# Down projection as seven block products in a hybrid-mixer layer on one core

## The chip, the core and the metric

The kernel runs on one core of a Trainium2 chip, as one program. Its engines are TensorE (PE, with PEld for its weight loads), VectorE (DVE), ScalarE (ACT), GpSimd (POOL) and the queue of SyncE (SP), which issues the DMAs of the kernel. The metric is the device time of one execution in microseconds, the median of several runs; lower is better.

## The reference

One layer of a diffusion backbone with 1024 tokens and 1024 channels: modulated norm, three token mixers (window attention, global attention, a two-way recurrence), a gated merge, an output projection, and then a gated feed-forward part with a depthwise convolution. What the change touches is the last product:

```python
def conv_ffn(h, w_up, w_dw, b_dw, w_down):
    a, g = jnp.split(dwconv(h @ w_up, w_dw, b_dw), 2, axis=-1)
    return (a * jax.nn.silu(g)) @ w_down          # (1024, 2816) @ (2816, 1024)
...
x = x_mix + m_lat[:, :, 5] * conv_ffn(h, ...)
return rms_norm(x, norm_final)
```

Everything is in float32.

## The kernel before

**Number format.** A float32 operand of a product is split into a high part, rounded to the fp32r format of TensorE, and a low part, the rest. A product is then three matmuls: high by high, high by low, low by high (`dn`, lines 982 to 985). The high part is a cast on ACT, the low part a subtraction on DVE (`split`, lines 735 to 737, for activations; `w_unit`, lines 155 to 168, for weights).

**Who sets the order.** The program is written as straight code; a planner then orders the instructions of each engine by a priority, which is the place in the code, lowered by an offset where `tc.high_priority(offset)` stands. It takes whatever is ready with the lowest number and puts in the semaphores. Tiles of one tag share a few buffers, and an instruction that needs a buffer waits until its last reader is done. Each engine then runs its own list in order. Weights go through three tags with three buffers each (`WR`, `WH`, `WL`): `wr` the raw float32 tile, `wh` and `wl` its two parts. Loads and stores are issued on SP.

**Global attention** (`attention` with `br` = 1, lines 1287 to 1427, in stage lines 683 to 691). Sixteen iterations `it`, one for 128 tokens and four heads. In iteration `it` three pieces of work are interleaved on PE: the scores of iteration `it + 1` (`softmax_global`, line 1469), the values of iteration `it` (`values`, line 1355: transposes `pp` of the probabilities, their split `ph` and `pl`, products `po`), and a filler, the gate projections (`gz`), whose weights come through `w_unit`. POOL has one instruction in an iteration: it copies the reciprocals of the softmax sums, widened, into a tile `rb` (line 1504, kept in `rs`). Two matmuls of `values` read that tile (`pr`, line 1372).

**Up projection** (lines 824 to 953). It is already done as seven block products for each pair of column tiles (Strassen's scheme in Winograd's form), with sums of weights made on POOL (lines 889 to 896). The activations that come out, 22 tiles of 128 by 1024, are stored to DRAM (`act_d`).

**Down projection** (lines 959 to 1077). The 2816 rows of the weights are 22 row tiles f, the 1024 output channels are 8 column tiles, the 1024 tokens two halves `tb`. The first half is done in two passes over all f (four column tiles in each, in four PSUM banks), the second half in one such pass and then column tile by column tile, with the last column tile cut into 384 and 128 tokens (`LAST`), so that the final norm of the first piece runs beside the matmuls of the second. In a pass a weight unit holds two row tiles by 512 columns, so that PE does 24 matmuls for one unit. Activations are loaded as half tiles `st` (four buffers), split, and the parts kept in a ring of 25 places (`ac`), from which both passes of the first half read. When a pass is done, DVE adds the PSUM banks, scaled, to the residual tile `xt` (`out_tile`), ACT squares the result, and POOL or DVE adds the squares for the final norm (`sumsq`).

## Time and profile before

| | |
|---|---|
| median of 3 runs | 2111.61 us (2109.61 to 2113.57) |
| the profiled execution, its own time | 2108.34 us |
| its span, first to last instruction | 2106.5 us |
| PE, PEld busy | 2068.0 us (98%), 1730.7 us (82%) |
| DVE, ACT, POOL busy | 1375.5, 1000.8, 287.1 us |
| granted TensorE clock | 0.998 of full speed |
| global attention | about 890 to 1190 us from the start of the span |
| up projection | 1415 to 1844 us |
| down projection | 1844 us to the end |

The profile is one execution, with all times counted from the first instruction. A row of the timeline has the start, the duration, the engine, the line of the code, the operation, the tile written and the tiles read, the shape, and in brackets how long the engine stood idle before it and what ended that. Durations of matmuls overlap, since they are pipelined: the distance of their starts is the pace. A row of a tile has the shortest, median and longest duration in nanoseconds, and the first and the last start. In a row of stretches stand the length, the busy time of each engine with its number of instructions, the granted clock, the share of the DMA engines' time and GB/s.

### The profile page before, as it was taken

Reading aid. Unit: us, or ns where it says so; the run is one execution under the profiler, and the core shown is the slowest. Engines: PE = TensorE matmul, PEld = TensorE weight load, DVE = VectorE, ACT = ScalarE, POOL = GpSimd, SP = SyncE. Lnnn points to the kernel's source line nnn. Section 1 sums busy time; section 2 is a strip of 40 time slices with the busy share of each in tenths; the row PEclk is TensorE's granted clock in tenths of the full one; section 3 lists DMA queues with packets and bytes.
Section 4 is the critical chain, followed back from the end, with each engine's and each line's share of the span. In section 5 each row is a group of like instructions: output and inputs, shape, how many; then the busy total and the mean of one; then the engine's idle time right before and its main releaser. Section 6 shows DMA issues by size and latency. Waiting matters only on the chain.

```text
span 2106.5 us, 30452 instructions
## 1 busy us (share of the span) xinstructions
PE 2068.0 (98%) x11666; PEld 1730.7 (82%) x11666; DVE 1375.5 (65%) x2280; ACT 1000.8 (48%) x1749; POOL 287.1 (14%) x257
## 2 busy tenths in 40 slices
PE   8999999999999999999999999999999999999997
PEld 5888888888988888778888788878888888888887
DVE  4846656636675788588888747569777777664423
ACT  4333333311123877688888634346544454453322
POOL 0000000010021222100000000011333334100111
PEclk9999999999999999999999999999999999999999
DMA  9311111136544211311010454641222222295342
GB/s 370 133 45 37 35 51 41 46 126 210 185 143 139 78 51 48 96 33 36 32 32 28 153 179 141 201 150 59 92 80 80 90 80 81 83 310 191 106 122 85
DMA packets 94338, 225.48 MB, mean 107 GB/s; under 512 B 10608, under 2 KB 35568, under 8 KB 93168
## 3 DMA queue, kind: packets, MB, share of 16 engines
q1 hardware_dynamic: 94192, 223.53, 32.0%
q8 instruction: 92, 1.51, 0.3%
q14 instruction: 54, 0.44, 0.1%
HBM read 177.88 MB, written 45.61 MB: 106 GB/s over the span
## 4 chain that ended last, share of the span: by engine, by line
PE 70%; DVE 2%; ACT 2%; issue 1%; POOL 1%; DMA 1%; SPq 0%; DVEq 0%; ACTq 0%; POOLq 0%
PE pp L1377 4%; PE gz L188 3%; PE gz L189 3%; PE dn L984 3%; PE dn L985 3%; PE dn L983 3%; PE gz L190 3%; PE up L907 2%; PE up L909 2%; PE up L908 2%; PE po L1363 2%; PE po L1364 2%; PE br L189 2%; PE br L190 2%; PE br L188 2%; PE upc L909 2%
## 5 line engine op out<-in xcount | busy, mean ns | idle before, releaser
L164 ACT CAST wh<-wr 128x1024 fp32r<-128x1024 f32 (+1 forms) x139 | 145.1, 1045 | 394.8 <-PE dn L984 72.6
L165 DVE TENSOR_TENSOR wl<-wr,wh 128x1024 fp32r<-128x1024 f32 (+1 forms) x139 | 171.2, 1232 | 217.6 <-ACT wh L164 214.4
L1382 DVE TENSOR_TENSOR pl<-pp,ph 128x512 fp32r<-128x512 f32 x236 | 159.7, 688 | 29.4 <-ACT ph L1381 23.7
L188 PE MATMUL gz<-hh,wh 128*128 128x512 f32 x384 | 155.4, 405 | 2.9 <-ACT gs L578 2.9
L189 PE MATMUL gz<-hl,wh 128*128 128x512 f32 x384 | 151.7, 395 | 0.0
L190 PE MATMUL gz<-hh,wl 128*128 128x512 f32 x384 | 151.6, 395 | 0.0
L1381 ACT CAST ph<-pp 128x512 fp32r<-128x512 f32 x236 | 135.5, 585 | 32.0 <-PE pp L1377 29.2
L199 PE MATMUL tm<-wl,hh 128*128 128x256 f32 x384 | 108.9, 283 | 2.4 <-DVE wl L165 2.4
L198 PE MATMUL tm<-wh,hh 128*128 128x256 f32 x384 | 108.7, 283 | 0.0
L200 PE MATMUL tm<-wh,hl 128*128 128x256 f32 x384 | 108.6, 283 | 0.0
L1363 PE MATMUL po<-ph,VHL 128*128 128x512 f32 x236 | 106.2, 450 | 1.5 <-ACT ph L1381 1.1
L984 PE MATMUL dn<-ac,wh 128*128 128x512 f32 x256 | 99.7, 390 | 0.0
L985 PE MATMUL dn<-ac,wl 128*128 128x512 f32 x256 | 99.6, 389 | 0.0
L983 PE MATMUL dn<-ac,wh 128*128 128x512 f32 x256 | 99.6, 390 | 0.0
L1364 PE MATMUL po<-pl,VHL 128*128 128x512 f32 x236 | 97.6, 413 | 0.1
L188 PEld LDWEIGHTS gz<-hh,wh 128*128 128x128 f32 x384 | 72.3, 188 | 16.3 <-ACT gs L578 5.0
L190 PEld LDWEIGHTS gz<-hh,wl 128*128 128x128 f32 x384 | 72.2, 188 | 15.0
L189 PEld LDWEIGHTS gz<-hl,wh 128*128 128x128 f32 x384 | 72.5, 189 | 11.2
L1377 PE MATMUL pp<-ident,plat 128*128 128x128 f32 x512 | 76.6, 273 | 0.0
L1377 PEld LDWEIGHTS pp<-ident,plat 128*128 128x128 f32 x512 | 62.8, 140 | 16.9 <-DVE pl L1382 1.2
L199 PEld LDWEIGHTS tm<-wl,hh 128*128 128x128 f32 x384 | 73.7, 192 | 3.3 <-DVE wl L165 3.0
L188 PE MATMUL br<-yh,wh 128*128 128x512 f32 x192 | 74.3, 390 | 1.2 <-ACT yh L1522 1.2
(1419 smaller groups left out, 5862.8 us busy)
## 6 DMA issues: line engine op xcount, KB each, us to landing
wr<-in_w_cm SPq DMA_DIRECT2D x48, 512.0 KB, 3.8
wr<-in_w_up SPq DMA_DIRECT2D x44, 512.0 KB, 3.5
wr<-in_w_down SPq DMA_DIRECT2D x33, 512.0 KB, 3.6
wmr<-in_w_mod SPq DMA_DIRECT2D x32, 512.0 KB, 4.6
gate_d<-gs SPq DMA_DIRECT2D x48, 256.0 KB, 2.1
sgt<-gate_d SPq DMA_DIRECT2D x24, 512.0 KB, 3.5
act_d<-u SPq DMA_DIRECT2D x22, 512.0 KB, 2.6
st<-act_d SPq DMA_DIRECT2D x44, 256.0 KB, 4.2
```

Source lines behind the costliest of these rows:

```text
L164: A.copy(hi[:, :n], raw[:, :n])
L165: (lo_eng or V).tensor_tensor(out=lo[:, :n], in0=raw[:, :n], in1=hi[:, :n].bitcast(F32), op=ALU.subtract)
L188: T.matmul(psl, wh[:, k, c], hh[:, k0 + k, cols], start=s, stop=False)
L189: T.matmul(psl, wh[:, k, c], hl[:, k0 + k, cols], start=False, stop=False)
L190: T.matmul(psl, wl[:, k, c], hh[:, k0 + k, cols], start=False, stop=e)
L199: T.matmul(psl, hh[:, k, toks], wl[:, k % 4, :], start=False, stop=False)
L983: T.matmul(z, w[0][:, c], h[0], start=s, stop=False)
L984: T.matmul(z, w[0][:, c], h[1], start=False, stop=False)
L985: T.matmul(z, w[1][:, c], h[0], start=False, stop=e)
L1363: T.matmul(po, vv, ph, start=n == 0, stop=False)
L1377: T.transpose(pp[:, h], PT(h, n), ident)
L1382: V.tensor_tensor(out=pl, in0=pp, in1=ph.bitcast(F32), op=ALU.subtract)
```

## The change

The down projection becomes seven products of blocks of half the size in each dimension: 11 row tiles, four column tiles, 512 tokens. With activations A and weights W in four blocks each, the products are, in this order, A11 with W11 (into PSUM set 0), a sum of activations with a sum of weights `T1` (into set 1), A12 with W21 (on top of set 0), another with the sum `22` (on top of set 1), one with `T2` (set 0 anew), one with `T3` (set 1 anew), and one with the plain block `T4`, which goes column tile by column tile as the second half did before. After each of the first six, DVE adds the set, scaled, to one, two or three groups of four residual tiles (`after`), so that both residual halves are in use from the first product on.

The sums of weights don't depend on the data. They are made in the global attention: after each iteration a step of the generator `down_sums` adds up on POOL what the last step loaded, stores the four results to DRAM (`s_d`) from POOL's queue, takes one `wr` and one `wl` buffer, writes one column of each from the tile `rb` of the next iteration, and loads the four blocks of the next row tile into them, on POOL's queue too.

The sums of activations are made on POOL in the down projection, in place, in raw tiles that stay in SBUF: 33 raw half tiles (15 in `p2`, 8 in `pa`, 10 in the five buffers of the tag `c`), and 11 more (`r`) that go through two buffers of the tag `st`. The split parts go through a ring of 12 places. The two weight arrays of the down projection become one, `w_dn`, cut into blocks with rows of 512 columns; an input that was not read, and a debugging output, are gone.

```diff
+        s_d = dt_([4, KD, P, 512], "s_d")
+        def down_sums():
+            last = None
+            turn = yield
+            for k in range(KD + 1):
+                if last is not None:
+                    (a11, a12), (a21, a22) = ((t[:, 0], t[:, 1]) for t in last)
+                    G.tensor_tensor(out=a22, in0=a21, in1=a22, op=ALU.add)
+                    G.tensor_tensor(out=a21, in0=a11, in1=a21, op=ALU.subtract)
+                    G.tensor_tensor(out=a11, in0=a22, in1=a11, op=ALU.subtract)
+                    G.tensor_tensor(out=a12, in0=a12, in1=a11, op=ALU.subtract)
+                    for j in range(2):
+                        G.dma_start(s_d[2 * j:2 * j + 2, k - 1].rearrange("a p c -> p a c"), last[j])
+                if k < KD:
+                    last = []
+                    for j in range(2):
+                        t = wp.tile([P, 2, 512], F32, tag="wrwl"[2 * j:2 * j + 2], name=f"sw{j}_{k}", bufs=WR if j == 0 else WL)
+                        G.tensor_copy(t[:, 0, 0:1], turn[:, 0:1])
+                        G.dma_start(t, ins["w_dn"][2 * j:2 * j + 2, k].rearrange("a p c -> p a c"))
+                        last.append(t)
+                turn = yield
...
-        NRING = 25
+        NRING = 12
+        prods = (("11", ins["w_dn"][0], 0, True), ("T1", s_d[3], 1, True), ("21", ins["w_dn"][1], 0, False),
+                 ("22", s_d[1], 1, False), ("T2", s_d[0], 0, True), ("T3", s_d[2], 1, True),
+                 ("T4", ins["w_dn"][3], 0, True))
...
+        def act(q, k):
+            j = (q * KD + k) % NRING
+            t = pa.tile([P, 2, LH], F32R, tag=f"ac{j}", name=f"ac{q}_{k}")
+            h = t[:, 0], t[:, 1]
+            with tc.high_priority(offset=APRIO):
+                if q == 0:
+                    split(h, raw(0, k))
+                elif q == 1:
+                    less(raw(0, k), raw(1, k), raw(0, k))
+                    split(h, raw(0, k))
+                elif q == 2:
+                    split(h, raw(2, k))
+                elif q == 3:
+                    r = p2.tile([P, LH], F32, tag="st", name=f"st{k}", bufs=2)
+                    SP.dma_start(r, act_d[KD + k][:, t2])
+                    split(h, r)
+                    less(raw(1, k), r, raw(1, k))
+                    less(raw(0, k), r, raw(0, k))
+                    less(raw(2, k), raw(2, k), raw(0, k))
+                else:
+                    split(h, raw((0, 1, 2)[q - 4], k))
+            return h
...
+        after = (((1, 0, 0), (0, 4, 0), (1, 4, 0)), ((1, 4, 0),), ((0, 0, 1),), ((1, 0, 0),),
+                 ((1, 0, 1), (0, 4, 0), (1, 4, 0)), ((1, 4, 1), (0, 4, 0)))
...
+        for q, (bn, src, st, new) in enumerate(prods[:-1]):
...
+            for k0 in range(0, KD, 2):
+                nk = min(2, KD - k0)
+                w = w_unit(src[k0:k0 + nk].rearrange("f p t -> p f t"), nk, 512)
+                for k in range(k0, k0 + nk):
+                    h = first.pop(0) if first else act(q, k)
+                    for j in range(4):
+                        dn(zs[j], [p[:, k - k0] for p in w], slice(j * P, (j + 1) * P), h, new and k == 0, k == KD - 1, **on)
...
+            for tb, i0, end in after[q]:
+                for j in range(4):
+                    add(tb, i0 + j, zs[j])
+                    if end:
+                        done(tb, i0 + j, count[tb])
...
+                for f0 in range(0, KD, 8):
+                    nk = min(8, KD - f0)
+                    if f0 not in ws:
+                        ws[f0] = w_unit(src[f0:f0 + nk, :, i * P:(i + 1) * P].rearrange("f p c -> p f c"), nk, P)
+                    for k in range(f0, f0 + nk):
+                        if k not in hs:
+                            hs[k] = act(q, k)
+                        dn(z, [p[:, k - f0] for p in ws[f0]], slice(0, P), [t[:, z0:z0 + n] for t in hs[k]],
+                           k == 0 and z0 == 0, k == KD - 1, **on)
```

At the end of iteration `it` of `attention`, where `extra` is `down_sums()` in the global one:

```diff
+        if extra is not None and it + 1 < n_it:
+            if it == 0:
+                next(extra)
+            extra.send(rs[it + 1])
```

`KD` is 11, half of `FT`; `less(out, a, b)` is a subtraction on POOL; `add` scales a PSUM tile and adds it to the residual tile on DVE; `done` is the square and its sum, as in `out_tile` before. The last loop shown is the seventh product, for column tile `i` and `n` tokens.

## The prediction

> **What bounds the kernel now.** I read the page first, then busy time by stage, then the starts of single matmuls, then who waits for whom in the down projection and in the global attention.

> ```profile
> PE 2068.0 (98%) x11666; PEld 1730.7 (82%) x11666; DVE 1375.5 (65%) x2280; ACT 1000.8 (48%) x1749; POOL 287.1 (14%) x257
> PEclk9999999999999999999999999999999999999999
> ```
> ```profile
> core 0: us, PE busy (x) PEld busy (x) DVE busy (x) ACT busy (x) POOL busy (x), PEclk, DMA share, GB/s
> 1016.00:1072.00 56.00, 55.66 (x326) 46.02 (x324) 45.53 (x77) 46.47 (x99) 1.20 (x3) 1.00 0.10 32
> ...
> 1844.00:1900.00 56.00, 55.99 (x248) 46.03 (x247) 34.87 (x41) 27.92 (x39) 0.00 (x0) 1.00 0.91 315
> 1900.00:1960.00 60.00, 60.00 (x267) 49.67 (x266) 28.83 (x34) 24.76 (x35) 4.94 (x3) 1.00 0.51 164
> 1960.00:2027.00 67.00, 67.00 (x311) 55.95 (x310) 23.95 (x25) 15.62 (x19) 6.70 (x5) 1.00 0.39 123
> ```
> PE is the bound everywhere, at the full granted clock. In the down projection (the last three rows) it has no gap, DVE is busy 62% and then less, POOL hardly at all; only the DMA engines are near full, and only in its first 56 us. In the global attention (first row, three iterations of 18.7 us) PE is full too, DVE is at 81% and POOL nearly idle. So a matmul that goes away in the down projection is worth its pace, if its operands keep coming.

> The busy column holds overlapping latencies (0.39 us each); the pace is the distance of starts:
> ```profile
> 1855.04 0.39 PE L983 MATMUL dn<-ac,wh 128*128 128x512 f32 x1
> ...
> 1899.92 0.39 PE L983 MATMUL dn<-ac,wh 128*128 128x512 f32 x1
> ```
> ```profile
> 2082.28 0.33 PE L983 MATMUL dl<-ac,wh 128*128 128x384 f32 x1
> ...
> 2084.18 0.33 PE L985 MATMUL dl<-ac,wl 128*128 128x384 f32 x1
> ...
> 2084.41 0.27 PE L984 MATMUL dl<-ac,wh 128*128 128x128 f32 x1
> ...
> 2086.87 0.28 PE L985 MATMUL dl<-ac,wl 128*128 128x128 f32 x1
> ```
> 198 matmuls of 512 columns lie between the first two rows: 44.88 / 198 = 0.2267 us. Eleven of 384 columns take 1.90 us, 0.173 each; 22 of 128 take 2.46, 0.112 each.

> [...]

> **The matmuls.** Before: three passes of 22 x 4 x 3 = 264, then three column tiles of 66 and a last one of 66 + 66 (384 and 128 columns): 1122. After: six products of 11 x 4 x 3 = 132, three tiles of 33 and 33 + 33: 957. Gone are 99 of 512, 33 of 384, 33 of 128 columns: 22.4 + 5.7 + 3.7 = **31.8 us**, all of it on the path.

> **The end.** The 66 narrow matmuls cover the norm of the first 384 columns; 33 remain.
> ```profile
> 2084.55 0.62 DVE L1065 SCALAR_TENSOR_TENSOR xt<-dl,mods,xt 128x384 f32<-128x384 f32 x1 [0.98 <-PE dl L985]
> ...
> 2090.22 0.86 POOL L248 TENSOR_TENSOR rsfl<-rsfl,mhalf 128x3 f32<-128x3 f32 x1 [29.17 <-DVE rsfl L247]
> ...
> 2093.68 0.29 PE L258 MATMUL rpf<-ident,rsfl 128*128 128x128 f32 x1
> ```
> From the wide chunk's last matmul (2084.4) the power is ready 6.7 us later, and PE reaches the transposes that read it at 9.3. With 3.7 us of matmuls gone PE reaches them at 5.6 and waits for the power: 1.1 us come back. **+1**.

> **Splits, adds, weights.** 33 more activations are cast and split, 49 reads of a PSUM set replace 17, weight units go from 48 to 44. Per row tile k, PE takes 12 x 0.2267 = 2.72 us.
> ```profile
> L737 DVE TENSOR_TENSOR ac<-st,ac x44: 678/691/715, 1849.9 to 1957.2; 128x512 fp32r<-128x512 f32 x44
> L165 DVE TENSOR_TENSOR wl<-wr,wh x47: 948/1225/2235, 1840.2 to 2085.2; 128x1024 fp32r<-128x1024 f32 x42, 128x768 fp32r<-128x768 f32 x5
> L989 DVE SCALAR_TENSOR_TENSOR xt<-dn,mods,xt x12: 741/751/752, 1903.5 to 2028.4; 128x512 f32<-128x512 f32 x12
> ```
> DVE's part per k is 0.69 + 1.225 / 2 + 49 x 0.75 / 77 = 1.78 us, 65% of 2.72: no bound by itself. The largest group of adds, 12 after the first product, is 9.0 us; the second product runs 29.9 us on the other PSUM set meanwhile. Without that cover it would cost the 9.0. ACT was half idle (27.92 of 56) and gets 33 more casts; hidden. **0**.

> **POOL's sums in the down projection.** 11 in the second product, 33 in the fourth ("22"), which also loads each r through two buffers; two sums must read r before its buffer is free.
> ```profile
> 1705.57 1.29 POOL L896 TENSOR_TENSOR s<-wr,s 128x512 f32<-128x512 f32 x1
> 1706.20 1.75 DVE L737 TENSOR_TENSOR wa16l<-wr,wa16h 128x1024 fp32r<-128x1024 f32 x1 [2.97 <-ACT wa16h L736]
> 1706.82 2.28 POOL L942 TENSOR_TENSOR c<-c,c 128x512 f32<-128x512 f32 x1
> ```
> These rows of the up projection show the price: a POOL sum alone takes 1.29 us; a DVE subtraction of two SBUF tiles that is issued beside it (1706.20) ends 1.09 us after POOL's end (1706.86 to 1707.95), and the next POOL sum, issued at 1706.82, ends 1.15 after that. The two take turns. So one k of the fourth product holds the turn for 3 x 1.29 + 1.30 = 5.17 us against PE's 2.72: 27.0 us too much over 11 k, if nothing runs ahead. What runs ahead:
> ```profile
> L977 SPq DMA_DIRECT2D st<-act_d x44: 319/320/430, 1841.8 to 1947.1; - x44
> ...
>   PE dn L985: 12.4, 9
> ...
> DMA to landing us min/median/max: 2.5/4.2/6.4
> ```
> Loads and splits of the second half stood waiting for PE to free a ring slot (12.4 us in 9 waits), so they run as far ahead as the ring lets them, here 12 tiles, a whole product. Over the third and fourth product (59.8 us) the turn is asked for by DVE 22 x 1.30 = 28.6, by 33 sums 42.6 and by three sums of squares 3.9: 75.1. The sums of k 0 and 1 can be done earlier, those of k 9 and 10 later (3.87 each): 59.6. It just fits. Ends 0 and 27; nearest is the fit, less some loss: **+3**. No gain is possible, as nothing leaves POOL or DVE here. The second product's 11 sums (14.2) have two products of room: 0.

> **Loads at the start of the stage.** All 33 raw tiles have places of their own, and the 16 residual tiles are asked for sooner.
> ```profile
> 1843.67 3.01 SPq L1035 DMA_DIRECT2D xt<-xm_d  x4
> ```
> That row shows loads that are needed late going out as soon as the queue has nothing else. In two products the stage needs 22 raw tiles, 12 residual tiles (0.262 MB each) and 14 weight units (0.524 each, three of them ahead): 16.2 MB, 52 us at the 315 GB/s above, of 59.8. The third block and four residual tiles (3.9 MB, 12 us) come on top and may stand ahead of a weight unit in SP's queue. Weights are asked for some three units (16 us) ahead. Ends 0 and 10; nearest is nothing, since PE had no gap at 0.91 DMA share: **+1**. The 512 B rows of the last product's weights touch 8 units with 5.4 us of PE each, behind six buffers: 0.

> **Weight sums in the global attention.** Per iteration, for 11 iterations: four POOL sums (5.2 us), two one-column copies, two loads and two stores of 0.5 MB issued on POOL, and one raw and one low weight buffer of three each held. DVE has few operations with two SBUF tiles there, so the turn matters little. Behind a POOL instruction that waits for a buffer or a load stands the copy of the softmax reciprocals:
> ```profile
> 1029.40 0.40 POOL L1504 COPY yT_r__10277<-st__10127 128x256 f32<-128x256 f32 x1 [18.00 <-PE pq L1342]
> ```
> ```profile
> L1372 PE MATMUL pr<-ident,yT_r__10277 x4: 275/275/348, 1034.0 to 1034.4; 128*128 128x128 f32 x4
> ```
> It is ready at 1029.8, and PE needs it at 1034.0: 4.2 us of room, three sums' worth. The buffers have room too:
> ```profile
> 908.89 0.33 SPq L161 DMA_DIRECT2D wr<-in_w_branch  x1
> ...
> DMA to landing us min/median/max: 3.4/3.5/5.3
> ```
> At 908.89, at the beginning of this stage, the weights of the next one are already being loaded; holding one buffer of three shortens that lead only. No POOL-issued DMA is in this trace; nearest are SP's (0.33 us to issue, 3.5 to 5.3 to land). Between 0 (all inside 4.2 us) and 69 (below), nearest is the first: some sums or DMA issues in front of a copy, 0.3 us an iteration, **+3**. Nothing is removed there, so no gain. The SP queue gets nothing new in this stage.

> **Sum.** -31.8 + 1 + 0 + 3 + 1 + 3 = -23.8 us on an execution of 2108.3 us (span 2106.5): 2084.5. That execution lies 3.3 below the median of 2111.6, so for the median **2088**.

> **Rivals.**
> *The fourth product runs at the pace of the turn.* If the r loads don't run ahead, 27 instead of 3 are lost: 2112. For it: two r buffers, and DVE is in order, so a split that waits for r holds the weight splits. Against it: the ring-bound waits above. Chance 0.13, half of it a partial loss.
> *Weights stand behind early loads.* 10 instead of 1 at the start: 2097. For: the xt row; against: no gap at 315 GB/s. 0.10.
> *The attention waits on POOL (slower).* If POOL stands before its sums until the loads land, with the copy behind it: 5.3 + 5.2 - 4.2 = 6.3 us an iteration, 69 over 11: 2088 - 3 + 69 = 2154. It decides from 27 / 11 = 2.4 us per iteration on. For: POOL is in order, and PE takes the reciprocals at a fixed place; against: the room of 4.2 us and 18.7 us per iteration for 5.2 of sums. 0.12. [...]
> *The products save fewer matmuls than counted*: the up projection's seven products already run gapless, so I give it nothing.

> **Chances.** My case 0.65, its own range 2079 to 2097. A measurement tells about 0.2% (4.2 us) from no change: 2107.4 to 2115.8 is "same". Faster: 0.65 + 0.10 + half of 0.13, and a little of the attention case below its limit: 0.83. Same 0.07, slower 0.10. Range 2077 (the full 31.8, and the lowest run's 2 us below the median) to 2106: it leaves out the attention case and half of the first rival.

> **What would show it.** Matmuls of the down projection 957 at 0.227 us. In the fourth product, PE gaps ended by DVE's ac or by a load of the r tile tell of the turn; gaps in the first product ended by wh or a DMA, of the loads; gaps before the pr matmuls ended by POOL, of the attention. The end after the last matmul should be about as long as now. The forecast fails if the sums of one product can't be done in another, or if POOL's own loads take far longer than SP's.

## The result and the profile after

The changed kernel takes 2114.9 us (median of 20 runs, 2108.9 to 2118.9), the kernel before 2110.2 in the same series: a ratio of 1.0022, 95% interval [1.0015, 1.0029]. It is 0.2% slower, where 2088, 1.1% faster, was forecast. The profiled execution has a span of 2114.4 us against 2106.5. One execution of the run fourth_in_order below took 5224.6 us, and its row is the median of the other nine.

From the page of the changed kernel, busy time by engine and two rows of the 40 slices (3 busy tenths means 30% of that slice):

```profile
PE 2052.1 (97%) x11501; PEld 1706.2 (81%) x11501; DVE 1437.9 (68%) x2339; ACT 1010.5 (48%) x1776; POOL 453.4 (21%) x411
POOL 0000000010021222134441000011233433326512
PEclk9999999999999999999999999999999999999999
```
The 165 saved matmuls are gone (11666 to 11501) and PE's busy time fell by 16, yet the span grew. POOL went from 287 to 453 us, in two places: the global attention (slices 18 to 22) and the down projection. I cut the span at the first matmul of each stage (score matmuls of the global attention, branch matmuls, down projection) and at its last one:

| stretch | before | after | difference | predicted |
|---|---|---|---|---|
| up to the first score matmul | 889.3 | 890.8 | +1.5 | 0 |
| global attention | 294.1 | 313.4 | **+19.3** | +3 |
| branches, merge, up projection | 661.1 | 661.7 | +0.6 | 0 |
| down projection | 249.1 | 234.1 | **-15.0** | -27.8 |
| end | 12.9 | 14.4 | +1.5 | +1 |

Busy time in the attention, first the changed kernel, then the kernel before (columns: span; PE, its weight loads, VectorE, ScalarE, POOL; clock; DMA):

```profile
890.80:1204.20 313.40, 298.59 (x1679) 239.11 (x1679) 253.70 (x394) 242.31 (x518) 99.76 (x126) 0.99 0.33 114
```
```profile
889.30:1183.40 294.10, 291.22 (x1681) 238.58 (x1681) 236.55 (x394) 241.07 (x518) 6.42 (x16) 1.00 0.12 37
```
VectorE has as many instructions as before (394) and is 17 us longer busy with them. The group that grew is the 128x1 minimum in each softmax row block. Four of them in one iteration, before and after (duration in ns, min/median/max):

```profile
L1494 DVE TENSOR_TENSOR st__9913<-st__9913 x4: 149/150/159, 999.4 to 1008.1; 128x1 f32<-128x1 f32 x4
```
```profile
L1568 DVE TENSOR_TENSOR st__9968<-st__9968 x4: 150/316/1620, 1005.4 to 1015.1; 128x1 f32<-128x1 f32 x4
```
The same iteration of the changed kernel in order of time shows why:

```profile
1007.91 1.30 POOL L695 TENSOR_TENSOR sw<-sw 128x512 f32<-128x512 f32 x1
```
```profile
1007.62 1.62 DVE L1568 TENSOR_TENSOR st__9968<-st__9968 128x1 f32<-128x1 f32 x1
```
An operation on one column ends at 1009.24, when POOL's sum ends (1009.21). The exponential on ScalarE (`plat`) waits for that minimum. PE waits for the exponential, or for the splits of the probabilities (`pl`) that stand behind the minimum on VectorE. In the rows below, of the changed kernel, stand who waited, for whom, the total in us, the number of waits and the longest:

```profile
PE pp L1447 <- DVE pl L1452: 6.4, 8, 3.7
...
PE sbl L1563 <- ACT plat L1570: 1.4, 2, 1.1
```
```profile
ACT plat L1570 <- DVE st__9517 L1568: 3.3, 3, 2.6
```
The first row was 0 in the kernel before; its longest wait, 3.7, has another cause, found below. All 64 minima take 24.4 us instead of 9.9; the 14 scaled subtractions of the queries, which also read two SBUF tiles, 10.0 us (718 ns each) instead of 6.3 (15, 419 ns each).

In the down projection the first two products and the last two of 512 columns run at pace, 29.9 us each (the first 30.2); the third and fourth take 74.9 instead of 59.9. Who waits there, in the changed kernel from 1940 to 2000 us:

```profile
ACT ac L763 <- DMA st<-act_d: 22.4, 7, 5.4
DVE ac L764 <- ACT ac L763: 18.5, 8, 5.0
...
ACT ssf L755 <- POOL ssf L760: 7.1, 1, 7.1
...
PE dn L1037 <- ACT wh L166: 5.5, 3, 4.2
...
PE dn L1039 <- DVE wl L167: 4.0, 3, 1.5
```
PE never waits for an activation. It waits for weights, whose casts stand on ScalarE behind casts of r that wait for their load. The loads of r wait in SyncE's queue for a buffer that POOL's sums still read (1865 to 2000 us):

```profile
SPq L1027 <- POOL raw L1011: 26.7, 8, 5.0
```

### The profile page after: what moved, and what is told of

Its sections match the earlier page's. It is cut to its first block, busy times and chain, and to the rows that moved or that the text cites. A ratio compares the mean times of both kernels' runs of the same rounds, so it can differ in the third digit from the quotient of the medians.

```text
span 2114.4 us, 30408 instructions
## 1 busy us (share of the span) xinstructions
PE 2052.1 (97%) x11501; PEld 1706.2 (81%) x11501; DVE 1437.9 (68%) x2339; ACT 1010.5 (48%) x1776; POOL 453.4 (21%) x411
## 4 chain that ended last, share of the span: by engine, by line
PE 62%; DVE 5%; POOL 3%; ACT 3%; issue 2%; DMA 1%; POOLq 0%; DVEq 0%; SPq 0%; ACTq 0%
PE pp L1447 3%; PE gz L190 3%; PE gz L191 3%; PE gz L192 3%; PE up L934 2%; PE up L935 2%; PE up L936 2%; PE dn L1039 2%; PE dn L1038 2%; PE dn L1037 2%; POOL raw L1011 2%; PE po L1433 2%; PE po L1434 2%; PE br L191 2%; PE br L192 2%
## 5 line engine op out<-in xcount | busy, mean ns | idle before, releaser
L166 ACT CAST wh<-wr 128x1024 fp32r<-128x1024 f32 (+2 forms) x135 | 137.3, 1017 | 334.4 <-PE gz L191 51.0
L167 DVE TENSOR_TENSOR wl<-wr,wh 128x1024 fp32r<-128x1024 f32 (+2 forms) x135 | 168.6, 1250 | 141.4 <-ACT wh L166 138.0
L1447 PEld LDWEIGHTS pp<-ident,plat 128*128 128x128 f32 x512 | 62.1, 141 | 26.7 <-DVE pl L1452 13.5
L191 PE MATMUL br<-yl,wh 128*128 128x512 f32 x192 | 75.1, 391 | 0.7 <-DVE yl L1597 0.7
```

The lines of the kernel that those rows point to most:

```text
L167: (lo_eng or V).tensor_tensor(out=lo[:, :n], in0=raw[:, :n], in1=hi[:, :n].bitcast(F32), op=ALU.subtract)
L191: T.matmul(psl, wh[:, k, c], hl[:, k0 + k, cols], start=False, stop=False)
L1447: T.transpose(pp[:, h], PT(h, n), ident)
```

## The experiments

The ratio is to the kernel before in the same series. Stage lengths are those of the one profiled execution: att. is the global attention, down the down projection (first to last matmul), loss what the third and fourth product take beyond 59.9 us.

| run | time, us | ratio to before | att. | down | loss |
|---|---|---|---|---|---|
| the change | 2114.9 | 1.0022 [1.0015, 1.0029] | 313.4 | 234.1 | 15.0 |
| att_no_sums | 2098.6 | 0.9952 [0.9937, 0.9967] | 298.5 | 233.3 | 14.2 |
| att_min_one_source | 2106.3 | 0.9985 [0.9976, 0.9994] | 303.9 | 234.1 | 15.1 |
| third_sum_later | 2114.9 | 1.0029 [1.0019, 1.0038] | 310.9 | 234.2 | 15.1 |
| fourth_in_order | 2114.8 | 1.0031 [1.0016, 1.0045] | 312.9 | 233.3 | 14.2 |
| fourth_no_sums | 2097.1 | 0.9941 [0.9926, 0.9956] | 311.2 | 219.1 | 0.0 |
| five_r_buffers | 2116.5 | 1.0031 [1.0019, 1.0044] | 313.9 | 235.8 | 16.6 |
| third_sum_last | 2118.0 | 1.0038 [1.0023, 1.0053] | 313.3 | 236.4 | 17.3 |
| min_and_raw_buffers | 2099.7 | 0.9955 [0.9940, 0.9970] | 298.2 | 234.0 | 14.9 |
| third_sum_dve | 2097.3 | 0.9936 [0.9923, 0.9948] | 298.2 | 232.4 | 13.3 |
| two_sums_dve | 2091.3 | 0.9908 [0.9893, 0.9923] | 298.1 | 228.5 | 9.4 |
| before_min_one_source | 2109.5 | 0.9998 [0.9989, 1.0007] | 293.8 | 249.1 | - |
| two_dve_five_r | 2092.4 | 0.9921 [0.9908, 0.9934] | 298.2 | 226.2 | 7.1 |
| one_dve_five_r | 2097.2 | 0.9942 [0.9930, 0.9955] | 298.1 | 233.1 | 14.0 |
| r_sums_dve_five_r | 2090.9 | 0.9909 [0.9896, 0.9922] | 298.2 | 224.5 | 5.4 |
| r_sums_dve_two_r | 2087.9 | 0.9897 [0.9884, 0.9910] | 298.6 | 222.5 | 3.3 |

**Attention: the sums or their transfers?** att_no_sums takes the four sums out of `down_sums`.

```
-                    G.tensor_tensor(out=a22, in0=a21, in1=a22, op=ALU.add)
...
-                    G.tensor_tensor(out=a12, in0=a12, in1=a11, op=ALU.subtract)
```

> The changed kernel with the four sums per iteration of the global attention left out (the weight blocks are still loaded into the same tiles and stored as they came, so the down projection multiplies with unsummed weights). Theory A, the sums on POOL take turns with VectorE's small two-tile operations (the 128x1 minimum took 0.155 us alone and 0.82 us beside a sum): the stage from the first score matmul to the first branch matmul falls from 313.4 us to about 296, the 128x1 minima are all near 0.155 us, and the time falls by 17 to 20 us to about 2096. Rival B, it is POOL's loads and stores, their descriptors or the weight buffers held by them: the stage stays at 310 or more and the time at about 2114.

The stage falls by 14.9 us, to 298.5, and the time by 16. The loads, stores and buffers were all still there: it was the sums, either by the turn or by how long they hold buffers, which this run does not separate.

**Is it the second SBUF source?** att_min_one_source keeps the sums and gives the minimum one source, a tile in which both columns are neighbours (nc_ is its second column).

```
-        V.tensor_reduce(out=n1, in_=sf, axis=AX.X, op=ALU.max, negate=True)
-        V.tensor_tensor(out=n1, in0=n1, in1=nc_[:, h:h + 1], op=ALU.min)
+        V.tensor_reduce(out=two[:, h, 0:1], in_=sf, axis=AX.X, op=ALU.max, negate=True)
+        V.tensor_reduce(out=n1, in_=two[:, h], axis=AX.X, op=ALU.min)
```

> The changed kernel with the 128x1 minimum of two SBUF columns made as a reduction over two neighbouring columns of one tile (one source instead of two). Theory A (turn-taking of operations with two SBUF sources): the minimum stays near 0.16 us beside a sum, the attention stage falls from 313.4 to about 299 (what stays is qs_q and wl beside a sum, and the PE gaps they make), the time by 12 to 17 us to about 2100. Rival A2, any VectorE operation in SBUF waits for POOL's sum: the reduction takes 0.8 us beside one and nothing moves, 2114. Rival B (loads, stores, buffers): the minimum gets fast and the time stays at 2114.

The same four minima there:

```profile
L1569 DVE TENSOR_REDUCE st__9968<-st__9968 x4: 141/146/155, 1002.7 to 1011.3; 128x1 f32<-128x2 f32 x4
```
All 64 now take 157 ns or less, beside a sum too, and the stage falls by 9.5 us, to 303.9, less than the 14 expected; the time falls by 8.6. What stayed was one large gap on PE of 4.4 us, and before it on VectorE:

```profile
1125.00 1.22 DVE L167 TENSOR_TENSOR wl<-wr,wh 128x1024 fp32r<-128x1024 f32 x1 [4.89 <-DMA s_d<-sw]
```
A weight split waited for the store of a sum out of the low buffer that it needs, and every later instruction of VectorE stood behind it. before_min_one_source, the same edit in the kernel without sums, is the control:

> The kernel before with the 128x1 minimum of the global attention made as a reduction over two neighbouring columns. No POOL sums run there, so theory A (the minimum is slow only beside a POOL sum) expects nothing: 2110, the attention stage 294. If the form by itself is better, the stage falls by 2 us or more, and part of what att_min_one_source gained was not the turn.

No difference (0.9998), so the gain was the turn and not the form. min_and_raw_buffers holds two raw buffers instead of a raw and a low one:

```
-tag="wrwl"[2 * j:2 * j + 2], ... bufs=WR if j == 0 else WL
+tag="wr", ... bufs=WR
```

> att_min_one_source (2106 measured) with both tiles of the weight sums in raw weight buffers (two of three) instead of one raw and one low buffer. Theory: the one large gap that is left in the attention there, 4.4 us with a half-clock stretch behind it, stands behind a weight split on VectorE that waited 4.9 us for the store out of a low buffer; with no low buffer held VectorE no longer stands, the stage falls from 303.9 to about 298 and the time by 5 to 6 to about 2101. Rival: with one raw buffer left the weight loads come late in that stage, PE waits for wh instead, 2106 or more.

The gap is gone; 298.2 and 2099.7, as expected. So the 15 us that att_no_sums gained are two things, the minima (9.5) and the held low buffer (5.7). The 4.1 us above the kernel before are there with or without the sums (298.5); in r_sums_dve_two_r below 2.6 of them are PE gaps ahead of score matmuls that end with ScalarE's copy of the scores, not with POOL. Their cause stays open.

**Down projection: POOL's sums, or something else?** fourth_no_sums leaves the three sums of the fourth product out.

```
-                    less(raw(1, k), r, raw(1, k))
-                    less(raw(0, k), r, raw(0, k))
-                    less(raw(2, k), raw(2, k), raw(0, k))
```

> The changed kernel with the three sums of each k in the fourth product left out (T2, T3 and T4 then multiply unsummed activations). Theory C (r buffers come free at the pace of POOL's sums, 4.4 us per k, and weight loads on SP and weight casts on ACT stand in line behind the r loads and casts that wait for them): the third and fourth product take 59.9 us instead of 74.9, no half clock there, the time falls by 15 to about 2100. Rival D (the round trip of r through two buffers by itself, landing time and order, whatever POOL does): at least 8 of the 15 us stay, 2107 or more.

All 15 us go. The two r buffers cost nothing when POOL does not read them. Both products in one row of that run:

```profile
1920.95:1981.10 60.15, 60.15 (x267) 49.84 (x266) 37.28 (x46) 27.36 (x40) 4.54 (x3) 1.00 0.46 142
```
Three runs tried to relieve POOL or the order and did not:

```
third_sum_later:  less(raw(2, k), raw(2, k), raw(0, k)) moved from q == 3 to q == 4
third_sum_last:   the same moved to q == 6, outside of the raised priority
fourth_in_order:  with tc.high_priority(offset=0 if q == 3 else APRIO):
```

> The changed kernel with the third sum of each k of the fourth product (raw2 - raw0, which reads no r) made one product later, just before raw0 is split for T2. Theory C (the two r buffers come free at the pace of POOL's sums, 4.4 us per k, and what stands behind the r loads on SP and ACT comes late): POOL needs about 3 us per k, the fourth product's 15 us of loss fall to under 5, the time falls by 9 to 14 us to about 2103. Rival D (the order on ACT and SP, which puts r loads and casts ahead of weights whatever POOL does, or the landing time of r): no change, 2114. Rival E (the sums only move): the fifth or last product loses what the fourth gains, 2112 to 2114.

> The changed kernel with the third sum of each k (raw2 - raw0) made at normal priority with the last product's activations, which are its only reader. In third_sum_later POOL made these sums between the others all the same (12 ring tiles of run-ahead allowed it), so POOL's load did not move; here the ring keeps them behind the fifth product. Theory C: POOL needs 2 x 1.5 = 3 us per k in the fourth product, the loss of 15 us falls to 0 to 6, the time to about 2104. Rival E (the loss only moves): the sixth product or the last waits for POOL instead and the time is 2111 or more.

> The changed kernel with the activations of the fourth product taken in program order instead of 60 instructions' priority ahead. Theory D (r casts that wait for a buffer stand ahead of the weight casts on ACT): weights come in time, the loss of 15 us in the fourth product goes to under 5, the time falls to about 2101. Theory C (the sums' pace sets it, 4.4 us per k against PE's 2.72): without the run-ahead PE waits for the split r instead, gaps end with ac rather than wh, and the time is 2114 or up to 10 us more.

None of them did what its edit says. In third_sum_last POOL still made the third sums between the others; the scheduler takes what is ready, and raw2 and raw0 were. From 1926 to 1984 us there:

```profile
L1011 POOL TENSOR_TENSOR raw<-st,raw 128x512 f32<-128x512 f32 x22 | 35.2, 1628 | 20.4 <-DMA st<-act_d 20.4
L1011 POOL TENSOR_TENSOR raw<-raw,raw 128x512 f32<-128x512 f32 x11 | 18.8, 1725 | 0.2
```
33 sums in 54 us without a pause, as in the change itself (35.3 and 18.9). In fourth_in_order ScalarE's line is the same, one or two r casts between every two weight casts. So these three say nothing for or against theory C (the sums' pace holds r's buffers, and what stands behind r comes late); a place in the program is not a place in an engine's line.

**More r buffers.** five_r_buffers: `NRING = 11`, `bufs=5`.

> The changed kernel with five buffers for r instead of two, and 11 ring tiles instead of 12 to make room. Theory C: POOL's pace stays 4.4 us per k, but r loads and casts no longer wait for it at the head of SP's and ACT's lines until late in the product; the loss of 15 us falls to 0 to 7, the time to about 2104. Rival T (the turn itself: VectorE's weight splits, 2.0 us instead of 1.2 beside a sum, are late whatever the buffers): gaps that end with wl stay and the time is 2112 or more.

Both theories miss: 16.6 us of loss, in one piece. ScalarE in that run:

```profile
1963.87 0.62 ACT L763 CAST ac<-raw 128x512 fp32r<-128x512 f32 x1
1983.88 0.63 ACT L755 ACTIVATE ssf<-xt 128x512 f32<-128x512 f32 x1 [19.39 <-POOL ssf L760]
1984.41 1.03 ACT L166 CAST wh<-wr 128x1024 fp32r<-128x1024 f32 x1
```
```profile
PE dn L1037 <- ACT wh L166: 12.2, 1, 12.2
```
The r loads now ran ahead, and ScalarE stood 4.3 us for them instead of 26.7 (1930 to 1996 us in both). But POOL's line was just as long, the adds of squares of the residual stood at its end, a fourth square waited 19.4 us for a buffer that they release, and the weight cast stood behind it. In the change the same wait is 7.1 us. From this comes theory P: what counts is how long POOL's line is.

**Shortening POOL's line.** From here on all runs build on min_and_raw_buffers.

```
third_sum_dve:      V.tensor_tensor(raw2 - raw0) with the last product's activations
two_sums_dve:       and V.tensor_tensor(r - raw1) in the fourth product
two_dve_five_r:     two_sums_dve with NRING = 11 and five r buffers
one_dve_five_r:     the third sum back on POOL (r - raw1 alone on VectorE)
r_sums_dve_five_r:  r - raw1 and r - raw0 on VectorE, the third sum on POOL
r_sums_dve_two_r:   the same with NRING = 12 and two r buffers, as in the change
```

> min_and_raw_buffers (2099.7 measured) with the third sum of each k of the down projection (raw2 - raw0) on VectorE, issued with the last product's activations. Theory P, formed from five_r_buffers: POOL's line is full from the first r to the end of the fourth product (33 sums of 1.5 us beside VectorE, and behind them three adds of squares, for which ACT stood up to 19.4 us with the weight casts behind it). With 11 sums of 1.5 off it POOL ends some 15 us sooner, the adds of squares come in time, the loss of 15 us in the third and fourth product falls to 0 to 5 and the time to about 2088. Rival T (the turn: what counts is the sum of two-source work on both engines, VectorE's weight splits get later by what it takes over): less than 5 us gained, 2095 or more.

> third_sum_dve with one of the two sums that read r (r - raw1) on VectorE as well, so POOL keeps one sum of three. Theory P: POOL is no longer full at all, the r buffers come free faster, the loss is gone: about 2086, or level with third_sum_dve if that one has none left. Rival T: VectorE, 0.69 us more per k in front of its weight splits, becomes late itself; gaps end with wl or ac and the time is above third_sum_dve by 3 us or more.

Theory P is half right. In third_sum_dve POOL's last sum ends at 1957.8 us instead of 1964.6 in min_and_raw_buffers, and the fourth square waits 0.7 us, yet only 1.6 us of the loss go. Who waits there from 1915 to 1980:

```profile
ACT ac L763 <- DMA st<-act_d: 30.4, 9, 7.1
POOL raw L1011 <- DMA st<-act_d: 11.7, 6, 5.7
...
PE dn L1041 <- DVE wl L167: 9.4, 2, 8.4
DVE raw L1034 <- POOL raw L1011: 7.8, 4, 2.9
```
POOL now waits for r, VectorE for POOL, and PE for a weight split. ScalarE waits for r longer than before, and that decides the 8.4 us gap, which ends at 1950.7:

```profile
1946.56 0.62 ACT L763 CAST ac<-st 128x512 fp32r<-128x512 f32 x1 [1.83 <-DMA st<-act_d]
1947.08 1.04 ACT L166 CAST wh<-wr 128x1024 fp32r<-128x1024 f32 x1
```
```profile
1948.36 2.28 DVE L167 TENSOR_TENSOR wl<-wr,wh 128x1024 fp32r<-128x1024 f32 x1
```
The weight cast stands behind r casts, and the split begins 0.24 us after the cast: VectorE's own wait for POOL costs no more than that there. two_sums_dve brings the loss to 9.4. For what was left the next four were run.

> two_sums_dve (2091.3 measured) with five r buffers and 11 ring tiles. There POOL was idle and waited for r, ACT stood up to 6.9 us for r loads, and PE had one gap of 7.2 us that ended with a weight split on VectorE. Theory R (what is left is the round trip of r through two buffers, with the weights in line behind it): with five buffers the gap goes, the loss of 9.4 us in the fourth product falls to 0 to 2, the time to about 2082. Rival X (VectorE, in order, waits for POOL's raw0 before its own third sum, with weight splits behind it): a loss of 5 us or more stays, 2087 or more.

> As two_dve_five_r, but the third sum (raw2 - raw0) back on POOL, which makes raw0 itself, so VectorE waits for POOL nowhere; VectorE keeps r - raw1. POOL then has 22 sums of about 1.5 us, 33 us, against 59.8 us of PE's third and fourth product. Theories R and X together: no loss, about 2082. If X alone mattered this is faster than two_dve_five_r; if POOL's line still makes the squares late (theory P), gaps end with wh behind ssf, 2088 or more.

> Both sums that read r on VectorE, the third on POOL, five r buffers and 11 ring tiles. r's buffers no longer wait for POOL at all. Theory R: no loss, about 2082. Rival T (the turn and VectorE's own load: 2 x 0.69 us more per k on VectorE before its weight splits): gaps ended by wl, 2086 or more.

> As r_sums_dve_five_r with the change's own two r buffers and 12 ring tiles. Theory P alone (POOL's pace was the whole of it): two buffers suffice once VectorE reads r right behind the split, about 2082, the same as with five. Theory R (the round trip through two buffers costs by itself): slower than r_sums_dve_five_r by 3 us or more, with gaps that end with weights behind r casts.

Theory R fails as a forecast: five buffers take the loss from 9.4 to 7.1 with one arrangement (the times, 2092.4 and 2091.3, do not differ) and from 3.3 to 5.4 with the other. Of those last 2.1 us about 0.6 are gaps and the rest matmuls at half clock (last section), and the intervals of the two times overlap. The five-buffer runs also have one ring place less, which no run separates. What R describes is in the trace all the same: in two_sums_dve the weight cast ahead of the 7.2 us gap stands behind an r cast that had waited 4.7 us for its load. With five buffers that wait is gone, and another takes its place: in two_dve_five_r the cast of the weight ends at 1939.6, and its split begins at 1942.8, behind four of VectorE's own sums. X alone falls too: one_dve_five_r, where VectorE waits for POOL nowhere, is the worst of the four (14.0), because there POOL has 22 sums again and VectorE's r sums take turns with them, 1672 ns each against 877 in two_sums_dve:

```profile
L1029 DVE TENSOR_TENSOR raw<-st,raw 128x512 f32<-128x512 f32 x11 | 18.0, 1672 | 0.1
```
```profile
L1029 DVE TENSOR_TENSOR raw<-st,raw 128x512 f32<-128x512 f32 x11 | 9.6, 877 | 2.2 <-DMA st<-act_d 2.2
```
Between two_sums_dve and r_sums_dve_two_r POOL has 11 sums both times and r two buffers. In the second POOL does not read r, and VectorE does not wait for POOL; no run separates these two. The loss goes from 9.4 to 3.3:

```profile
1910.20:1973.50 63.30, 60.55 (x267) 49.49 (x266) 58.71 (x66) 26.55 (x40) 29.05 (x14) 1.00 0.41 131
```
VectorE is at 93% there, and the 2.8 us of PE gaps end with its weight splits. This run beats both kernels: 2087.9 us, 1.0% below the kernel before. That it lies at the 2088 of the forecast is chance: it is another kernel, 4.5 us slower in the attention than the kernel before.

## Why the prediction was wrong, point by point

**Matmuls, -31.8: right.** With the fourth product's sums out the down projection takes 219.1 us, 30.0 less than before. Of the other 1.8, 1.2 are two gaps in the last product that end with VectorE's add of the tile before.

**The end, +1, and the loads at the start, +1: right or nearly.** The end grew by 1.5. The first product ran without a gap, so the loads cost 0.

**Splits and adds, 0: right** but for the 1.2 us above.

**Weight sums in the attention, +3: the main error, 19.3.** The step that failed is "DVE has few operations with two SBUF tiles there, so the turn matters little". I judged operations by their size. The minimum has one column and 0.15 us, but there are 64, each with ScalarE's exponential behind it, and any of them that falls beside a POOL sum can wait for the whole of it (21 of the 64 did fall beside one, 0.85 us in the mean). The price of the turn was in the prediction, taken from the up projection; it was not applied to this line. The trace has the price for this operation too: the 21 took up to 1.62 us (at 1007.62 us, with the whole of a 1.30 us sum inside), the other 43 at most 0.161. In att_min_one_source the `tensor_reduce` with one source took 0.157 us at most, beside a sum too.

The 4.2 us of room for the copy of the reciprocals was true and beside the point: no gap ahead of a pr matmul ended with POOL. POOL's own loads landed 4.0 to 5.5 us after the start of their issue, 4.6 in the median, against 3.8 for SP's weight loads of the same size in that stage; 0.74 of it is the issue on POOL, and no gap of PE ended with one of them. The slower rival had the right stage and the wrong wait. A smaller miss: "holding one buffer of three shortens that lead only" left out that VectorE, in order, stands in front of the held low buffer; that was 5.7 us.

**POOL's sums in the down projection, +3: the second error, 15.** "It just fits" was nearly true as a sum: POOL finished its 33 sums at 1982.5, and the third and fourth product, begun at 1926.0, would have ended without a gap at 1985.9. The step that failed is taking a fit of totals for a fit of deadlines, with loads that "run as far ahead as the ring lets them": that was read from a kernel in which these loads had four buffers and POOL read none of them, and here the loads waited 26.7 us for POOL. r casts and loads stood in ScalarE's and SP's lines ahead of weights that PE needed sooner, and the squares stood at the end of POOL's. The first rival (27 lost) named that order for VectorE; it came as half of that, on ScalarE first.

**A term that was missing: the clock.** PE's gaps in the third and fourth product add up to 9.6 us, the loss to 15.0. Of the other 5.4, 3.5 are 16 matmuls at half the clock behind the gaps. About 0.16 more comes with each gap, because the idle time is counted from the end of a matmul (0.39 us) and the next could have started after 0.227. I priced a gap at its own length.

The two errors, 16.3 and 12.0, make 28.3; the profiled execution (2116.2) came out 31.7 above the 2084.5 forecast for it. Of the other 3.4, 1.5 is the shift ahead of the attention, which is chance (last section), the rest the small rows above.

## What to carry to other kernels

Before two-source work goes to POOL, list every VectorE operation of that stage that reads two SBUF tiles, however small, and look at what stands behind it; here the minimum with two sources took up to 1.62 us beside a POOL sum, its one-source form 0.157 at most. When work is put ahead of its time, ask of each wait what is queued behind it on the same engine and when that is due, not only whether the totals fit. Count a PE gap of over two microseconds for more than its length: here the gap of 4.24 us in the fourth product was followed by 6.83 us at half the clock, the two of 1.02 and 1.26 us in one step by 3.41 (next section).

## What the runs showed of the hardware

```profile
1955.84:1959.25 3.41, 0.64 (x3) 0.19 (x1) 0.96 (x1) 0.15 (x1) 3.33 (x4) 1.00 0.50 148
1959.25:1966.08 6.83, 4.11 (x9) 2.81 (x10) 4.39 (x3) 2.03 (x3) 6.75 (x5) 0.50 0.22 79
1969.49:1972.90 3.41, 1.13 (x5) 0.39 (x3) 2.80 (x3) 1.67 (x3) 3.33 (x3) 1.00 0.37 132
1972.90:1976.31 3.41, 3.41 (x8) 2.66 (x9) 3.41 (x5) 3.41 (x7) 3.33 (x3) 0.50 0.62 154
```
```profile
1964.21 0.63 PE L1038 MATMUL dn<-ac,wh 128*128 128x512 f32 x1
1964.63 0.63 PE L1039 MATMUL dn<-ac,wl 128*128 128x512 f32 x1
```
In the half-clock steps the matmuls start 0.43 us apart instead of 0.227. Over all 17 profiles (the first 300 us and the end left aside), 38 of 41 half-clock stretches followed a step in which PE was idle 1.93 us or more in all (gaps over 0.05 us). The other three followed one with 1.3 to 1.6. No step with more than 1.95 us idle was followed by full clock. The idle time need not fill the step or be in one piece: in the third row above it is 2.28 of 3.41 us, in pieces of 1.02 and 1.26 us.

The steps have no fixed place in the kernel: counted back from the half-clock stretches, an edge falls on the first instruction in the profile of the change (within 0.01 us), and in that of the kernel before the first edge comes 1.70 us after it. So the same gap can cost more or less. Both kernels have a gap of 2.0 to 2.3 us that ends at about 590 us. In the kernel before an edge of the steps (counted back from the half-clock stretch at its end) cuts it into 0.95 and 1.08 us, and the clock stayed whole. In the change it lies in one step, and the next was halved, which is about the 1.5 us by which everything behind it is shifted (half of 3.41 is 1.7). All 17 profiles have this gap, 1.7 to 2.7 us long: the first score matmul starts at 888.2 to 890.1 us in the six with no halved step there, and at 890.4 to 892.7 in the other eleven, whatever the kernel. So single profiles differ by a step or two by chance. The time behind the gap, before and after:

```profile
589.87:593.28 3.41, 3.41 (x15) 2.84 (x16) 0.08 (x1) 0.00 (x0) 0.00 (x0) 1.00 0.72 246
```
```profile
590.50:593.91 3.41, 3.41 (x9) 2.66 (x9) 0.00 (x0) 0.00 (x0) 0.00 (x0) 0.50 0.64 240
```
